# VectorE's order in the second and third expert block: gate product and token low halves first, map building behind them, and the map results read one block later

## The chip, the core and the metric

One core of a Trainium2 chip runs the whole program. The metric is the device time of one execution in microseconds (us). The engines are named as in the profile: PE is TensorE's matmul, PEld its weight load, DVE is VectorE, ACT is ScalarE, POOL is GpSimd, SP is SyncE. Each engine has its own list of instructions; they meet through semaphores only.

## What is computed

A decoder layer on 512 tokens of width 1024: a hybrid mixer, a layer norm, a mixture of experts and a second layer norm. The change lies in the mixture of experts, which is, cut to what matters:

```python
def hierarchical_moe(x, w_rg, b_rg, w_re, b_re, w_up, w_down):
    """Top-1 expert group, then top-2 experts inside that group; SwiGLU experts."""
    xf = x.reshape(bsz * seq, d)
    ...
    gate = jnp.sum(jax.nn.one_hot(expert_id, N_EXPERTS) * weights[..., None], axis=1)
    h = jnp.einsum('nd,edf->nef', xf, w_up)
    h_g, h_u = jnp.split(h, 2, axis=-1)
    h = jax.nn.silu(h_g) * h_u * gate[:, :, None]
    y = jnp.einsum('nef,efd->nd', h, w_down)
```

There are 16 experts in 4 groups, each 1024 -> 2 x 256 -> 1024, and a token goes to two of them. All of it is in float32.

## The kernel before

**Arithmetic.** A float32 operand is split into a high half (rounded to the matmul's float32r, by a cast on ACT) and a low half (the rest, a subtraction on DVE). A product takes three matmul passes: high x high, high x low, low x high. So each weight tile needs a cast on ACT and a subtraction on DVE before PE can use it, and DVE's subtractions ("low halves") are most of its work.

**Blocks.** The experts run as 18 blocks of up to 128 tokens each, in the loop over `b`. The list `seq` names the expert of each block: 0, 1, 2, 3, 4, then 15 twice, 5, 14 twice, and so on. Blocks 0 to 4 have a fixed place in the tables (`NSTAT` = 5, "static"). From block 5 on, the tokens of a block are known only from the "dynamic maps" `ix_x` (which tokens) and `gw_x` (their gate weights), which have to be built on the chip while the first blocks run.

**One block b**, in the order in which the code issues it:

- `up_mm(b)`: 24 matmuls of PE on the tokens `xs` and the up weights `hl` (L109 in the profile, `mm<-hl,xs`).
- `h_ev`: the transposed hidden tile of block b-1 gets its high half (ACT) and its low half (DVE, L83 `hT`).
- `dn_prep`: the down weights of block b-1: casts L1200 (ACT), two low halves L1209 (DVE).
- Up weights of block b+1: four casts L761 (ACT) and four low halves L767 (DVE). Three of the low halves stand here, the fourth is put into the list `tail`.
- `gate_h`: the activation (ACT L1176), then the product with the gate weight (DVE L1177). I call it the gate product of block b.
- `transp(b+1)`: 8 transposes (PE L1162) of the gathered tokens of the next block and their halves (ACT and DVE L83 `xs`).
- `weave(tail)`: what was put into `tail`, on DVE.
- a gather (POOL L1086, an indirect DMA) for block b+4, and a scatter-add (POOL L1233) of an earlier block's result.
- `down_mm(b-1)`: 12 matmuls (PE L1220).
- `h_tr(b)`: two transposes of the hidden tile (PE L1183). They need the gate product of block b. `up_mm(b+1)` stands right behind them on PE.

`weave(chain, fill)` issues the operations of `chain` with those of `fill` spread between them. The stretch is scheduled by hand (`manual_schedule`): the order in the code is the order on each engine.

**The maps.** `order_experts` (L1126 to L1138) and `order_tokens` (L1281 to L1299) are some 30 small DVE operations on tiles of at most 128 x 160. `map_ops` builds the operands of a small matmul: `ohv_x` (L1045) and eight one-hot tiles (L1047). `map_mm` (PE L1055, 8 matmuls into a PSUM tile `aux`) multiplies them. `map_ix` (DVE L1061) turns the result into row numbers `ix_x`, which the gathers for block 5 and later need; `map_gw` (DVE L1066, L1067) gives `gw_x`, which the gate product needs from block 5 on. So DVE feeds `map_mm` and reads its result.

Of the kernel before, what the change touches and what calls it, by code (L numbers as in the profile page):

```python
# [34 lines left out]
NCOLX = NDYN + NSPLIT + NEXTRA  # L35
# [18 lines left out]
def trunk(ctx, tc, x, mem, rows, cols, wz, wkv, pac, pb8, pb2, wax, ws, wo, wr, br, we, out):  # L54
# [88 lines left out]
    def weave(chain, fill=()):  # L143
        done = 0
        for i, f in enumerate(chain):
            f()
            while done * len(chain) < (i + 1) * len(fill):
                fill[done]()
                done += 1
# [100 lines left out]
    with ExitStack() as st_a:  # L250
# [106 lines left out]
        rstd, ops = rstd_ops(mv)  # L357
# [51 lines left out]
        zx, ops = rstd_ops(None, 2, xst[:, :, 2])  # L409
# [87 lines left out]
    with ExitStack() as sc_stack:  # L497
# [15 lines left out]
        for h in range(CH):  # L513
# [19 lines left out]
            for et in range(2):  # L533
                ps = mmps()
                ztile(ps, wq, et)
                b = cc(C_Q + 2 * h + et)
# [227 lines left out]
    def prep_lo(key, i, eng=None, c0=0, c1=1024):  # L764
        t = wus[key][i]
        src = raws[key, i // 2][:, (i % 2) * 1024:(i % 2 + 1) * 1024]
        (eng or dve).tensor_tensor(t[:, 1, c0:c1], src[:, c0:c1], t[:, 0, c0:c1].bitcast(F32), op=ALU.subtract)  # L767
# [291 lines left out]
    def map_ix(ps_, nb, name):  # L1059
        ix = rtile([P, nb], "ix_" + name, I32)  # L1060
        dve.tensor_scalar(ix, ps_[:, :nb], -1.0, None, op0=ALU.add)  # L1061
        return ix
# [20 lines left out]
    def gather(key, ix, b):  # L1083
        xg = xgs[len(xgi) % len(xgs)]
        xgi[key] = xg
        pool.indirect_dma_start(out=xg, out_offset=None, in_=x1_d[:, :],  # L1086
                                in_offset=bass.IndirectOffsetOnAxis(ap=ix[:, b:b + 1], axis=0),
                                bounds_check=T - 1, oob_is_err=False)
# [7 lines left out]
    blk = {}  # L1096
# [164 lines left out]
    def where(b):  # L1261
        p_ = seq[b]
        if p_ < NSTAT:
            return ixs, gws, NS - 1 - p_
        second = b > 0 and seq[b - 1] == p_
        return blk["ixx"], blk.get("gwx"), p_ - NSTAT + (NSPLIT if second else 0)
# [38 lines left out]
    for b in range(nb):  # L1305
        p_ = seq[b]
        nxt = seq[b + 1] if b + 1 < nb else p_
        pu = up_mm(b)
        if b == 0:
            sp.dma_start(seen_d, xgi[1][0:1, 0:4])  # L1310
            for e, u in ((2, 1), (3, 0), (3, 1), (4, 0), (4, 1)):
                load_unit(e, u)
            dn_hi(0, 0)
            dn_hi(0, 1)
            pw = map_mm(ohs_s, NS, 1, 3)
            gws = map_gw(pw, NS, "s")
            h = gate_h(pu, gws, NS - 1)
            hT = h_ev(h_tr(h))
            dn_lo(0, 0, dve, None)
            transp(1)  # L1320
            dn_lo(0, 1, dve, None)
            pdn[0] = down_mm(0, hT)
            scatter(down_ev(pdn[0]), *where(0)[::2])
        elif b > 1:
            hT = h_ev(pth)
        if b == 3:
            blk["ixx"] = map_ix(pix, NCOLX, "x")
            gather(5, *where(5)[::2])
            gather(6, *where(6)[::2])
            weave(vals_x)  # L1330
            pwx = map_mm(ohs_x, NCOLX, 1, 3)
        if b == 4:
            blk["gwx"] = map_gw(pwx, NCOLX, "x")
        ix, gw, c = where(b)
        new = [seq[b - 1]] if b and (b == 1 or seq[b - 2] != seq[b - 1]) else []
        if b == nb - 1:
            break

        def dn_prep():
            for p1 in new:  # L1340
                pl = pools[p_] if nxt != p_ else xp if pools[p_] is hlp else hlp
                for n in range(2):
                    if b > 1:
                        dn_hi(p1, n)
                        dn_lo(p1, n, dve, pl)
                if at[p1] + 3 < E:
                    load_unit(order[at[p1] + 3], 2)

        if b == nb - 2:
            scatter(down_ev(pdn[b - 2]), *where(b - 2)[::2])  # L1350
        dn_prep()
        tail = []
        if b == 1:
            load_unit(order[5], 0)
        if b and nxt != p_:
            for i in range(3):
                prep_hi(nxt, i)
        if 3 < b < nb - 2:
            yb = down_ev(pdn[b - 2])
        held = b > 1 and seq[b - 2] == seq[b - 1]  # L1360
        if b and nxt != p_:
            if not held:
                prep_hi(nxt, 3)
            if b == 1:
                ops = oe_b + order_tokens()
                weave(ops[:8], [lambda i=i, c=c_: prep_lo(nxt, i, None, c, c + 512) for i in range(2) for c_ in (0, 512)])
                weave(ops[8:18], [lambda c=c_: prep_lo(nxt, 2, None, c, c + 512) for c_ in (0, 512)])
                tail = ops[18:] + [lambda: prep_lo(nxt, 3)]
            else:
                ops = []  # L1370
                if b == 2:
                    ohs_x, ops, vals_x = map_ops(blk["px"], blk["ohx"], NCOLX, "x")
                weave(ops[:5] or [lambda: None] * 3, [lambda i=i: prep_lo(nxt, i) for i in range(3)])
                tail = ops[5:] if held else ops[5:] + [lambda: prep_lo(nxt, 3)]
        if b and nxt != p_:
            for i in (2 * at[p_] + 9, 2 * at[p_] + 10):
                if i < 2 * E:
                    load_unit(order[i // 2], i % 2)
        if b:
            h = gate_h(pu, gw, c)  # L1380
        if 0 < b < nb - 1:
            transp(b + 1)
        weave(tail)
        if b + 4 < nb and b not in (1, 2):
            gather(b + 4, *where(b + 4)[::2])
        if b == nb - 2:
            gb2 = mlate.tile([P, 2048], F32, name="raw3")
            g2, b2 = gb2[:, :D], gb2[:, D:]

            def load_gb(eng, i):  # L1390
                r = ROWS.index("ln2_g") + i
                eng.dma_start((g2, b2)[i], rows[r:r + 1, :].to_broadcast([P, D]))

            load_gb(sp, 0)
            load_gb(sp, 1)
        if 3 < b < nb - 2:
            scatter(yb, *where(b - 2)[::2])
        if b == nb - 4:
            oht = mox.tile([P, 4, T], F32R, name="rawx", bufs=2)
            row_hot(oht[:, 0], *where(nb - 3)[::2])  # L1400
        if b == nb - 3:
            for i in range(1, 3):
                row_hot(oht[:, i], *where(nb - 3 + i)[::2])
        if b > 1:
            pdn[b - 1] = down_mm(b - 1, hT)
            if b == nb - 2:
                ys.append(down_split(pdn[b - 1]))
            elif b < 3:
                scatter(down_ev(pdn[b - 1]), *where(b - 1)[::2])
        if b:  # L1410
            pth = h_tr(h)
        if held:
            prep_half(nxt, 3)
        if b == 2:
            pix = map_mm(ohs_x, NCOLX, 0, 1)
    xz = yp.tile([P, NT, D], F32, name="y")
    xs_ = [xz[:, t, :] for t in range(NT)]
    for t in range(NT):
# [167 lines left out]
```

## Time and profile before

| | us |
|---|---|
| median of 3 runs | 917.89 (917.84 to 918.22) |
| the profiled execution, its own time | 920.99 |
| its span, from the first to the last instruction | 919.2 |

The profile is of one execution. Of its span PE is busy 96%, DVE 64% and ACT 50%. The stretch of the change lies between about 718 and 770 us of the span. "Granted clock" is the clock that PE got, as a share of 2.4 GHz: 1.00 is 2.4 GHz and 0.50 is 1.2 GHz. The chain of waits follows back from the last instruction to what released each step, and so lists what set the end. In a timeline row, the bracket says how long the engine had stood idle before that row, and what ended the wait.

### The profile page before, as it was taken

Reading aid. Unit: us, or ns where it says so; the run is one execution under the profiler, and the core shown is the slowest. Engines: PE = TensorE matmul, PEld = TensorE weight load, DVE = VectorE, ACT = ScalarE, POOL = GpSimd, SP = SyncE. Lnnn points to the kernel's source line nnn. Section 1 sums busy time; section 2 is a strip of 40 time slices with the busy share of each in tenths; the row PEclk is TensorE's granted clock in tenths of the full one; section 3 lists DMA queues with packets and bytes.
Section 4 is the critical chain, followed back from the end, with each engine's and each line's share of the span. In section 5 each row is a group of like instructions: output and inputs, shape, how many; then the busy total and the mean of one; then the engine's idle time right before and its main releaser. Section 6 shows DMA issues by size and latency. Waiting matters only on the chain.

```text
span 919.2 us, 11177 instructions
## 1 busy us (share of the span) xinstructions
PE 883.4 (96%) x4272; PEld 733.8 (80%) x4272; DVE 588.8 (64%) x1020; ACT 460.6 (50%) x656; POOL 58.1 (6%) x59
## 2 busy tenths in 40 slices
PE   9999999999999999999999999999998889999991
PEld 5778888889998888888878888788887678888870
DVE  6765773344555543345866865766768887689976
ACT  5545432223444342214678687534204657688942
POOL 0000100000000000000000000000001123233210
PEclk9999999999999999999999999999997989999996
DMA  8313632333322412221313322237673988899544
GB/s 339 123 46 115 218 126 97 112 112 109 121 93 92 142 46 91 102 79 73 129 62 106 138 73 88 92 109 279 229 286 112 409 320 274 269 285 405 146 151 96
DMA packets 29281, 144.70 MB, mean 157 GB/s; under 512 B 5461, under 2 KB 5717, under 8 KB 16166
## 3 DMA queue, kind: packets, MB, share of 16 engines
q1 hardware_dynamic: 21462, 127.25, 37.6%
q0 software_dynamic: 6048, 13.45, 5.8%
q10 hardware_dynamic: 1712, 3.24, 1.1%
q8 instruction: 35, 0.57, 0.3%
q14 instruction: 24, 0.20, 0.1%
HBM read 136.24 MB, written 17.30 MB: 167 GB/s over the span
## 4 chain that ended last, share of the span: by engine, by line
PE 78%; DVE 11%; ACT 5%; DMA 3%; issue 2%; SPq 0%; DVEq 0%; ACTq 0%
PE mm L109 61%; PE mm L1220 4%; PE aux L109 4%; PE mm L308 3%; DVE hl L767 2%; PE aux L1162 1%; DMA x<-in_x_dram 1%; DMA col<-in_cols_dram 1%; ACT hl L82 1%; PE aux L1442 1%; DMA o<-in_we_dram 1%; DVE hl L83 1%; PE aux L464 1%; DVE xs L83 1%; ACT hl L1200 1%
## 5 line engine op out<-in xcount | busy, mean ns | idle before, releaser
L109 PE MATMUL mm<-hl 128*128 128x512 f32 x1416 | 327.6, 390 | 0.2 <-DVE hl L83 0.2
L109 PEld LDWEIGHTS mm<-hl 128*128 128x128 f32 x1416 | 264.7, 188 | 54.6 <-DVE hl L83 0.6
L83 DVE TENSOR_TENSOR hl<-raw,hl 128x1024 fp32r<-128x1024 f32 (+1 forms) x116 | 136.3, 1181 | 136.7 <-ACT hl L82 136.2
L82 ACT CAST hl<-raw 128x1024 fp32r<-128x1024 f32 (+1 forms) x116 | 116.3, 1015 | 126.3 <-PE mm L109 113.8
L109 PE MATMUL mm<-o,hl 128*128 128x512 f32 x624 | 142.9, 389 | 1.2 <-ACT o L82 1.2
L109 PEld LDWEIGHTS mm<-o,hl 128*128 128x128 f32 x624 | 117.1, 188 | 25.8 <-ACT o L82 1.6
L109 PE MATMUL mm<-hl,xs 128*128 128x512 f32 x408 | 99.7, 401 | 0.0
L109 PEld LDWEIGHTS mm<-hl,xs 128*128 128x128 f32 x408 | 77.1, 193 | 15.9
L767 DVE TENSOR_TENSOR hl<-o,hl 128x1024 fp32r<-128x1024 f32 (+1 forms) x45 | 50.3, 1147 | 4.8 <-ACT hl L761 4.7
L1220 PE MATMUL mm<-hl,hT 128*128 128x512 f32 x196 | 49.5, 399 | 0.0
L761 ACT CAST hl<-o 128x1024 fp32r<-128x1024 f32 x42 | 41.9, 1051 | 4.2 <-PE mm L1220 4.2
L1220 PEld LDWEIGHTS mm<-hl,hT 128*128 128x128 f32 x196 | 35.6, 188 | 6.8
L1086 POOL DMA_INDIRECT y<-x_d,ixg x3 | 3.2, 1070 | 594.5 <-DVE rtl L1145 593.9
L224 ACT ACTIVATE gate<-mm,col 128x512 f32<-128x512 f32 x24 | 16.5, 688 | 39.7 <-PE mm L109 39.6
L1209 DVE TENSOR_TENSOR hl<-raw,hl 128x1024 fp32r<-128x1024 f32 x26 | 30.6, 1220 | 3.2 <-PE mm L109 1.6
L1200 ACT CAST hl<-raw 128x1024 fp32r<-128x1024 f32 x32 | 31.9, 1053 | 0.0
L109 PE MATMUL mm<-memT,hl 128*128 128x256 f32 x192 | 27.3, 286 | 0.2 <-ACT memT L82 0.2
L308 PE MATMUL mm<-o,hl 128*128 128x512 f32 x96 | 25.8, 421 | 0.9 <-ACT hl L82 0.6
L109 PEld LDWEIGHTS mm<-memT,hl 128*128 128x128 f32 x192 | 24.9, 191 | 0.9 <-ACT memT L82 0.4
L808 ACT COPY x1T<-aux 128x512 f32<-128x512 f32 x8 | 4.7, 587 | 40.6 <-PE aux L807 25.9
L109 PE MATMUL mm<-hl,yh 128*128 128x512 f32 x96 | 24.4, 400 | 0.0
L109 PE MATMUL mm<-hl,memT 128*128 128x256 f32 x192 | 24.3, 283 | 0.0
(337 smaller groups left out, 1157.8 us busy)
## 6 DMA issues: line engine op xcount, KB each, us to landing
raw<-in_wz_dram SPq DMA_DIRECT2D x30, 1024.0 KB, 4.7
o<-in_we_dram SPq DMA_DIRECT2D x21, 1024.0 KB, 8.0
raw<-in_we_dram SPq DMA_DIRECT2D x18, 1024.0 KB, 7.5
rawx<-in_we_dram SPq DMA_DIRECT2D x9, 1024.0 KB, 7.8
raw<-in_pac_dram SPq DMA_DIRECT2D x8, 1024.0 KB, 4.7
raw<-in_wkv_dram SPq DMA_DIRECT2D x8, 1024.0 KB, 4.7
raw<-in_pb_dram SPq DMA_DIRECT2D x4, 1024.0 KB, 6.2
raw<-in_wo_dram SPq DMA_DIRECT2D x4, 1024.0 KB, 4.9
```

What stands on the lines that cost most here:

```text
L82: act.copy(hi, src)
L83: dve.tensor_tensor(lo, src, hi.bitcast(F32), op=ALU.subtract)
L109: pe.matmul(ps, lhsT=a(sa_), rhs=b(sb_), start=first and i == 0, stop=last and i == 2)
L224: act.activation(store[j], ps, AF.Sigmoid, bias=cc(C_M + br_i * 8 + j))
L308: pe.matmul(ps, lhsT=xT(k, slice(t * P, (t + 1) * P))(sx), rhs=wv[2 * n + k // 4, k // 2 % 2][:, sw, k % 2, :], start=i == 0, stop=i == 23)
L464: pe.matmul(pv[:, ch * P:(ch + 1) * P], lhsT=v[:, ch, g * P:(g + 1) * P], rhs=wst[:, g, :], start=True, stop=True)
L761: act.copy(t[:, 0], raws[key, i // 2][:, (i % 2) * 1024:(i % 2 + 1) * 1024])
L767: (eng or dve).tensor_tensor(t[:, 1, c0:c1], src[:, c0:c1], t[:, 0, c0:c1].bitcast(F32), op=ALU.subtract)
L1162: pe.transpose(ps[:, j * P:(j + 1) * P], xg[:, k * P:(k + 1) * P], ident)
L1200: act.copy(dnh[key][:, :, n * 512:(n + 1) * 512], dn_half(key, n))
L1209: eng.tensor_tensor(dnl[key][n], dn_half(key, n), dnh[key][:, :, ns].bitcast(F32), op=ALU.subtract)
L1220: pe.matmul(ps, lhsT=hT[:, sa_, f, :], rhs=dn[sb_][:, f, :], start=i + f == 0, stop=i + f == 3)
```

## The change

Three things move; no operation is added or removed.

1. In block 1 the rest of `order_experts` and all of `order_tokens` but its first eight operations go from ahead of the gate product into `tail`, behind the low halves of up weight tiles 2 and 3.
2. In block 2 the making of the map operands (`ohv_x`, eight L1047), until now woven between the up weights' low halves, goes into `tail`, behind all four low halves.
3. `map_mm` for `ix_x` moves from the end of block 2 to behind `up_mm(3)`, with its reading `map_ix` right behind it. The other half (`vals_x`, `map_mm` for `gw_x`) moves from block 3 to behind `up_mm(4)`, with `map_gw` right behind it.

```diff
@@ -1324,12 +1324,12 @@
         if b == 3:
-            blk["ixx"] = map_ix(pix, NCOLX, "x")
+            blk["ixx"] = map_ix(map_mm(ohs_x, NCOLX, 0, 1), NCOLX, "x")
             gather(5, *where(5)[::2])
             gather(6, *where(6)[::2])
+        if b == 4:
             weave(vals_x)
             pwx = map_mm(ohs_x, NCOLX, 1, 3)
-        if b == 4:
             blk["gwx"] = map_gw(pwx, NCOLX, "x")
@@ -1364,14 +1364,13 @@
             if b == 1:
                 ops = oe_b + order_tokens()
                 weave(ops[:8], [lambda i=i, c=c_: prep_lo(nxt, i, None, c, c + 512) for i in range(2) for c_ in (0, 512)])
-                weave(ops[8:18], [lambda c=c_: prep_lo(nxt, 2, None, c, c + 512) for c_ in (0, 512)])
-                tail = ops[18:] + [lambda: prep_lo(nxt, 3)]
+                tail = [lambda i=i: prep_lo(nxt, i) for i in (2, 3)] + ops[8:]
             else:
-                ops = []
+                weave([lambda: None] * 3, [lambda i=i: prep_lo(nxt, i) for i in range(3)])
+                tail = [] if held else [lambda: prep_lo(nxt, 3)]
                 if b == 2:
                     ohs_x, ops, vals_x = map_ops(blk["px"], blk["ohx"], NCOLX, "x")
-                weave(ops[:5] or [lambda: None] * 3, [lambda i=i: prep_lo(nxt, i) for i in range(3)])
-                tail = ops[5:] if held else ops[5:] + [lambda: prep_lo(nxt, 3)]
+                    tail += ops
@@ -1411,8 +1410,6 @@
         if held:
             prep_half(nxt, 3)
-        if b == 2:
-            pix = map_mm(ohs_x, NCOLX, 0, 1)
```

How the lists of instructions change, at three places. First DVE in block 1, as a piece of the difference (`h<-h,gw_s,mm` is the gate product of block 1, `xs` the token low halves of block 2, `hl<-o` low halves of block 2's up weights):

```order
 L1135 TENSOR_TENSOR tab<-ntot,nx 128x16
+L1177 SCALAR_TENSOR_TENSOR h<-h,gw_s,mm 128x256
+L83 TENSOR_TENSOR xs<-aux,xs 128x512 x2
+L767 TENSOR_TENSOR hl<-o,hl 128x1024 x2
 L1136 TENSOR_REDUCE eidf<-scr 128x7
-L767 TENSOR_TENSOR hl<-o,hl 128x512
 L1137 COPY eidf<-ntot 128x1
 L1138 TENSOR_SCALAR eix<-eidf 128x8
 L1281 TENSOR_TENSOR scr<-oh,tab 128x128 x2
 L1284 TENSOR_REDUCE t_5544<-scr 128x8
```

The gate product and the token low halves now stand ahead of the small operations from L1136 on.

Second, PE from the end of block 2 to block 4 (`aux<-ident,h` is `h_tr`, `aux<-ident,y` is `transp`, 128x20 is the map for `ix_x`, 128x40 that for `gw_x`):

```order
 L1183 MATMUL aux<-ident,h 128x128 x2
+L109 MATMUL mm<-hl,xs 128x512 x24
 L1055 MATMUL aux<-ohv_x,yb 128x20 x8
+L1162 MATMUL aux<-ident,y 128x128 x8
+L1220 MATMUL mm<-hl,hT 128x512 x12
+L1183 MATMUL aux<-ident,h 128x128 x2
 L109 MATMUL mm<-hl,xs 128x512 x24
 L1055 MATMUL aux<-ohv_x,yb 128x40 x8
```

Each of the two map matmuls now stands one `up_mm` later than before.

Third, DVE from block 3 on, first as it was:

```order
L83 TENSOR_TENSOR hT<-aux,hT 128x256
L1061 TENSOR_SCALAR ix_x<-aux 128x20
L1045 TENSOR_TENSOR ohv_x<-ohx,val 128x8x20 x2
L1209 TENSOR_TENSOR hl<-raw,hl 128x2x512 x2
L767 TENSOR_TENSOR hl<-o,hl 128x1024 x3
L1177 SCALAR_TENSOR_TENSOR h<-h,gw_s,mm 128x256
L83 TENSOR_TENSOR xs<-aux,xs 128x512 x2
L767 TENSOR_TENSOR hl<-o,hl 128x1024
L83 TENSOR_TENSOR hT<-aux,hT 128x256
L1066 COPY gw_x<-aux 128x20
L1067 TENSOR_TENSOR gw_x<-gw_x,aux 128x20
L1209 TENSOR_TENSOR hl<-raw_5523,hl 128x2x512 x2
```

and as it is now:

```order
L83 TENSOR_TENSOR hT<-aux,hT 128x256
L1061 TENSOR_SCALAR ix_x<-aux 128x20
L1209 TENSOR_TENSOR hl<-raw,hl 128x2x512 x2
L767 TENSOR_TENSOR hl<-o,hl 128x1024 x3
L1177 SCALAR_TENSOR_TENSOR h<-h,gw_s,mm 128x256
L83 TENSOR_TENSOR xs<-aux,xs 128x512 x2
L767 TENSOR_TENSOR hl<-o,hl 128x1024
L83 TENSOR_TENSOR hT<-aux,hT 128x256
L1045 TENSOR_TENSOR ohv_x<-ohx,val 128x8x20 x2
L1066 COPY gw_x<-aux 128x20
L1067 TENSOR_TENSOR gw_x<-gw_x,aux 128x20
L1209 TENSOR_TENSOR hl<-raw_5523,hl 128x2x512 x2
```

On DVE the two reads of the maps, L1061 and L1066, keep their places in blocks 3 and 4, ahead of the down weights' low halves L1209, the up weights' low halves L767 and the gate product L1177 of the same block; what they read is now made by PE behind `up_mm` of the same block.

## Rows read from the trace of the kernel before

**Rows 1.** The page: span, then busy time (share of span) of PE.
```profile
span 919.2 us, 11177 instructions
PE 883.4 (96%) x4272; PEld 733.8 (80%) x4272; DVE 588.8 (64%) x1020; ACT 460.6 (50%) x656; POOL 58.1 (6%) x59
```

**Rows 2.** Timeline of PE, 722 to 775: start, duration, engine, line; idle before.
```profile
727.30 0.44 PE L1183 MATMUL aux<-ident,h 128*128 128x128 f32 x2 [2.17 <-DVE h L1177]
727.50 5.74 PE L109 MATMUL mm<-hl,xs 128*128 128x512 f32 x24
...
738.97 0.44 PE L1183 MATMUL aux<-ident,h 128*128 128x128 f32 x2 [2.12 <-DVE h L1177]
...
740.36 1.03 PE L1055 MATMUL aux<-ohv_x,yb 128*128 128x20 f32 x4 [0.59 <-DVE yb L1047]
```

**Rows 3.** Chain of waits, 715 to 920: start, us, what.
```profile
738.52 0.39 DVE h L1177
...
740.36 1.03 PE aux L1055 x4
741.39 7.99 PE mm L109 x24
749.38 0.80 PE aux L1055 x8
750.18 0.94 PE aux L1162 x8
751.12 2.79 PE mm L1220 x12
753.91 0.22 PE aux L1183 x2
754.12 5.48 PE mm L109 x24
...
763.23 0.22 PE aux L1183 x2
```

**Rows 4.** Windows of 1 us: PE, PEld, DVE, ACT, POOL busy; PEclk, DMA share, GB/s.
```profile
739.00:740.00 1.00, 0.77 (x6) 0.67 (x6) 1.00 (x2) 0.56 (x2) 0.80 (x1) 0.80 1.07 377
...
746.00:747.00 1.00, 1.00 (x5) 0.77 (x4) 1.00 (x2) 0.00 (x0) 0.00 (x0) 0.78 0.95 328
```

**Rows 5.** Timeline of all engines, 698 to 728 (first two) and 726 to 775.
```profile
723.79 0.17 DVE L1135 TENSOR_TENSOR tab<-ntot,nx 128x16 f32<-128x16 f32 x1
...
724.30 0.39 ACT L1176 ACTIVATE h<-mm 128x256 f32<-128x256 f32 x1 [1.11 <-PE mm L109]
...
734.02 0.32 DVE L1045 TENSOR_TENSOR ohv_x<-ohx,val 128x160 fp32r<-128x160 f32 x1
...
736.72 0.47 DVE L1047 TENSOR_SCALAR yb<-iof,px 128x128 fp32r<-128x128 f32 x2
```

**Rows 6.** Timeline of all engines, 711 to 715, DVE's part.
```profile
712.21 0.17 DVE L1066 COPY gw_s<-aux 128x6 f32<-128x6 f32 x1 [0.70 <-PE aux L1055]
...
714.10 0.42 DVE L83 TENSOR_TENSOR hT<-aux,hT 128x256 fp32r<-128x256 f32 x1 [0.94 <-ACT hT L82]
714.44 1.22 DVE L1209 TENSOR_TENSOR yb<-raw,hl 128x1024 fp32r<-128x1024 f32 x1
```

**Rows 7.** Timeline of all engines, 726 to 775, DVE's rows of blocks 3 and 4.
```profile
742.29 0.16 DVE L1061 TENSOR_SCALAR ix_x<-aux 128x20 int32<-128x20 f32 x1
...
744.24 2.36 DVE L1209 TENSOR_TENSOR hl<-raw,hl 128x1024 fp32r<-128x1024 f32 x2 [1.32 <-ACT hl L761]
...
746.52 3.49 DVE L767 TENSOR_TENSOR hl<-o,hl 128x1024 fp32r<-128x1024 f32 x3
...
749.92 0.47 DVE L1177 SCALAR_TENSOR_TENSOR h<-h,gw_s,mm 128x256 f32<-128x256 f32 x1
...
755.11 0.18 DVE L1067 TENSOR_TENSOR gw_x<-gw_x,aux 128x20 f32<-128x20 f32 x1
```

**Rows 8.** All instructions on the tile ix_x: its gathers and scatters to landing.
```profile
DMA to landing us min/median/max: 4.8/6.3/10.9
```

## The prediction

> **What bounds the kernel now.** I read the page first: PE is busy for 883.4 of 919.2 us [rows 1], so only what PE waits for can matter. The next view is PE's timeline through the expert blocks: where it stands idle, and on whom it waits. There are three waits between 725 and 741, each on DVE: 2.17 us ahead of `h_tr(1)`, 2.12 ahead of `h_tr(2)`, both for the gate product L1177, and 0.59 in the map matmul, for the one-hot tiles L1047 [rows 2]. From 741.39 on the chain of waits is PE alone, block after block [rows 3], so whatever is won or lost up to block 4 stays to the end. The third view is the windows of 1 us: the granted clock is 1.00 until 739.6 and 0.50 (1.2 GHz) from there to 746.4. I get the two instants from the mixed values, 0.80 and 0.78 [rows 4]: 0.5 for a share x of the microsecond gives 1 - x/2, so x is 0.4 in each. `up_mm(3)` lies in the slow stretch and takes 7.99 us, where `up_mm(4)` takes 5.48 [rows 3]. PE had just stood still for 2.12 us when the clock fell. After the 2.17 us ahead of block 2 it did not fall: `up_mm(2)` took 5.74 on the same timeline [rows 2], against 8.0 in the slow stretch.
>
> **Block 1.** DVE ends L1135 at 723.96, and ACT has the activation of block 1 at 724.69 [rows 5]. In the new order the gate product comes next, so it starts at about 724.7. It takes 0.39 [rows 3], and `h_tr(1)` goes at 725.15 instead of 727.30: 2.15 us won, PE's first wait gone. `up_mm(2)` moves up as much.
>
> **Block 2 gives it back.** DVE has no slack here: from 723.96 until the gate product of block 2 at 738.52 [rows 3, 5] it is busy throughout. The new order takes `ohv_x` (0.23 to the next start) and four one-hot tiles (0.39 for two [rows 5], so 0.8) out of that stretch: 1.0 us less. It adds 0.75 us in which DVE waits for the activation at 724.69, and the small operations, most of them depending on the one before, now run without a low half between them; I put 0.2 on that. That makes the gate product of block 2 come at about 738.5, as before. PE gets there earlier and waits longer, about 3 us in place of 2.1. So the 2.15 us are worth nothing by themselves.
>
> **The map matmul leaves its place.** Before, it stood between `h_tr(2)` and `up_mm(3)`; now `up_mm(3)` starts at 739.2 instead of 741.39. I let the clock fall at 739.6 and rise at 746.4 as before, since PE's wait ahead of it is longer, not shorter. By 739.6 0.4 us of the 5.48 are done, in the slow stretch 6.8 / 2 = 3.4, and the other 1.7 at full clock end at 748.1. Behind it comes the map matmul, 0.80 [rows 3] at full clock, to 748.9. In the old order this place held the other map matmul, from 749.38 on, so PE is 1.3 us ahead.
>
> **DVE stands still for the map, in block 3.** The order on DVE is `hT`, `map_ix`, two L1209, three L767, gate product. `map_ix` can't start before 748.9, while DVE is ready at about 743.5 (the last low half of block 2, nine map operations and `hT` behind 738.5: 0.4 + 1.2 + 1.15 + 1.9 + 0.35). What waits behind it is not only what needs the map. That DVE passes nothing ahead is shown by the low half L1209 at 714.44: its inputs were there while DVE stood idle for 0.70 and 0.94 us on other tiles, and it ran behind both [rows 6]. After the map DVE needs 0.17 for `map_ix`, 2.28 for two L1209 (744.24 to 746.52), 3.40 for three L767 (to 749.92 [rows 7]), 0.39 for the gate product: 6.3 us with the hand-overs, to 755.2. PE has 0.94 of transposes and 2.79 of `down_mm(2)` [rows 3], 3.7 us, and then waits 2.6. In the kernel before, the same 5.7 us of low halves ran from 744.24 on under `up_mm(3)`; that cover is gone. `h_tr(3)` comes at 755.2 instead of 753.91: 1.3 late.
>
> **The same again in block 4.** `up_mm(4)` takes 0.22 + 5.48 from there, to 760.9; the second map matmul 0.80, to 761.7 (it stood in block 3 before). `map_gw` is two small operations of about 0.2 [rows 7], so DVE needs 6.5 to the gate product, and `h_tr(4)` comes at 768.2. Before it came at 763.23 [rows 3]: 5.0 late. In this block PE waits 2.8. Nothing later gives it back: behind block 4 PE was already the only link of the chain.
>
> **The gathers** of blocks 5 and 6 need `ix_x` and go at 749.1 instead of 742.7. The slowest of its gathers and scatters landed 10.9 us after issue [rows 8], so by 760.0; `transp(5)` stands at 761.7. No wait. The weight loads are issued when low halves free their buffers, so they move with DVE by the same 5 us, and no ACT cast of blocks 3 to 15 waited for a load; I cost them at nothing.
>
> **The clock, the cost that has no row of its own.** Two new waits, 2.6 and 2.8 us, are longer than the one after which the clock held (2.17) and the one after which it fell (2.12, with the 0.59 soon after) [rows 2]. One fall costs up to 3.4 us: 6.8 us at half clock, if PE has work throughout, and `up_mm(4)` with what follows is such work; some of it is hidden where PE then waits for DVE anyway, so I take 3.3. From below the bound is nothing. I hold a fall behind either wait for a little likelier than not, and one fall in all for the likeliest.
>
> **The sum** against the profiled execution (920.99): 5.0 without a further fall, 8.3 with one, 11.6 with two. I carry these to the median. The median, 917.89, lies 3.10 below the profiled execution. That is close to what its fall at 739.6 cost (7.99 - 5.48 = 2.5, and 0.6 in the map matmul), so the timed runs may not have had this fall; the new order, with its wait of 3 us there, would then add it, which is the same one further fall.
>
> **The rivals.**
> - *No further fall*: 917.89 + 5.0 = 922.9. For it: PE stood 2.17 us at full clock without a fall.
> - *Two further falls*: 917.89 + 11.6 = 929.5. For it: both new waits are longer than any that kept the clock in these blocks.
> - *Faster*: `up_mm(3)` keeps 2.4 GHz, and DVE's low halves fit under PE. The place is the stretch from the map matmul to the gate product in blocks 3 and 4. `up_mm(3)` then ends at 744.7, the map at 745.5, `h_tr(3)` comes at 749.2 and `h_tr(4)` at 749.2 + 0.22 + 5.48 + 0.80 + 3.7 = 759.4: 3.9 won, 914.0. It decides from the point where DVE gets from the map to the gate product in 3.7 us rather than 6.3; the durations in rows 7 speak against it.
> - *Nothing*: the waits are covered, the clock falls as before. `h_tr(3)` at 752.6, `h_tr(4)` at 762.8: 0.4 won, 917.5. It would need the moved reads not to hold DVE up, which is the case in which the change does not do on DVE what its list says.
> - *The old fall goes*: DVE's waits stay, but the clock holds in `up_mm(3)`. Map at 745.5, `h_tr(3)` 751.8, `h_tr(4)` 764.8: 1.6 late, 919.5.
> - *Late gathers*: POOL issues them from 749.1 on beside DVE's unbroken low halves, where before DVE was idle until 744.24 [rows 7]. `transp(5)` waits from the point where a landing takes more than 12.6 us. If one came as far behind the slowest as that lies behind the median (10.9 + 4.6 = 15.5 [rows 8]), it would wait 2.9: 925.8. Against it: the gathers of this kernel ran beside DVE's low halves in most blocks and landed within 10.9. The Trainium skill's page "SBUF — State Buffer", section "SBUF: two separate sides", says that VectorE and GpSimd share a port pair as an exclusive lock, so that a DMA issued by GpSimd can wait for a VectorE instruction to end, and gives 620 ns alone against 3100 ns beside one. By an estimate from that page the slowest would land 2.5 us later, 0.8 behind the slack, and the time would be 923.7.
>
> **How the numbers follow.** Chances: one further fall 0.37, none 0.24, two 0.20, late gathers 0.02, old fall gone 0.06 (half of it within 0.2%), nothing 0.06, faster 0.05. A measurement of this kernel can tell about 0.2% (1.8 us) from no change. The likeliest is 917.89 + 8.3 = 926.2. The range from 921.5 to 930.5 holds no, one and two falls with about 1 us for my DVE times, and leaves out 0.17 and a small tail. Slower by over 0.2%: 0.37 + 0.24 + 0.20 + 0.02 + 0.03 = 0.86; within: 0.09; faster: 0.05.
>
> **What would show it.** In the profile after: `h_tr(1)` near 725.2 with no wait; the gate product of block 2 still near 738.5; DVE idle for some 5 us ahead of L1061, and again ahead of L1066, released by PE L1055; PE idle 2.6 to 2.8 us ahead of `h_tr(3)` and `h_tr(4)`, on DVE L1177; L1162 of block 5 without a wait. I am wrong if DVE runs L1209 and L767 of block 4 ahead of L1061, if the gate product of block 2 comes two or more us earlier, or if the clock behaves otherwise: each fall is a stretch at 0.50 of about 6.8 us.

## The result: slower by 5.3 us

| | before | after |
|---|---|---|
| median of 5 runs | 918.20 us (917.84 to 918.67) | 923.51 us (921.88 to 928.13) |
| profiled execution | 920.99 us, span 919.2 | 921.88 us, span 920.1 |
| mean granted clock of the profiled execution | 0.982 | 0.986 |

The ratio after to before is 1.0057, with an interval of 1.0041 to 1.0073: small, but clear of the noise. The time lies in the predicted range, 2.7 us below the predicted 926.2 and 0.6 above the 922.9 of the rival without a further clock fall. The two profiled executions lie only 0.9 us apart: the one of before is among its slowest (918.2 is its median), the one of after is its fastest. So the two traces must not be compared by their spans. I compare waits, and the distance from one `h_tr` to the next. Block 1 begins about 1.2 us earlier in the trace of after, because the stretch at 0.50 that both traces show near 700 us lasted 6.8 us in that execution and 10.2 in the one of before (`up_mm(0)` took 7.29 us against 8.59); instants of the two traces are not compared either. One of the six executions of the kernel after in the last experiment took 1779.23 us, at a granted clock of 1.00 and for a reason that the record doesn't show; it is counted in no figure below.

The page of after, the rows that answer to [rows 1]:

```profile
span 920.1 us, 11178 instructions
...
PE 882.1 (96%) x4272; PEld 732.3 (80%) x4272; DVE 588.3 (64%) x1019; ACT 460.5 (50%) x656; POOL 61.7 (7%) x59
```

PE, DVE and ACT have no more work than before (POOL has 3.6 us more, and is idle for 93% of the span), so the time was lost standing still. DVE even has one instruction fewer: the low half of up weight tile 2 in block 1, two operations of 512 columns before, is one of 1024 now, so the change doesn't only move things. The timeline of PE in after, 722 to 785 us, answers to [rows 2 and 3] (start, duration, engine, line, operation; in brackets the idle time before it and who ended that):

```profile
724.03 0.44 PE L1183 MATMUL aux<-ident,h 128*128 128x128 f32 x2
724.23 5.94 PE L109 MATMUL mm<-hl,xs 128*128 128x512 f32 x24
...
738.01 0.44 PE L1183 MATMUL aux<-ident,h 128*128 128x128 f32 x2 [2.83 <-DVE h L1177]
738.21 5.71 PE L109 MATMUL mm<-hl,xs 128*128 128x512 f32 x24
743.75 0.96 PE L1055 MATMUL aux<-ohv_x,yb 128*128 128x20 f32 x8
...
751.13 0.41 PE L1183 MATMUL aux<-ident,h 128*128 128x128 f32 x2 [2.70 <-DVE h L1177]
751.30 5.70 PE L109 MATMUL mm<-hl,xs 128*128 128x512 f32 x24
756.84 0.96 PE L1055 MATMUL aux<-ohv_x,yb 128*128 128x40 f32 x8
757.65 1.09 PE L1162 MATMUL aux<-ident,y 128*128 128x128 f32 x8
...
764.44 0.66 PE L1183 MATMUL aux<-ident,h 128*128 128x128 f32 x2 [2.90 <-DVE h L1177]
764.75 6.83 PE L109 MATMUL mm<-hl,xs 128*128 128x512 f32 x24
```

The four rows of L1183 are `h_tr(1)` to `h_tr(4)`. The wait of 2.17 us ahead of `h_tr(1)` is gone, the one ahead of `h_tr(2)` has grown from 2.12 to 2.83, and there are two new ones, 2.70 ahead of `h_tr(3)` and 2.90 ahead of `h_tr(4)`, all released by the gate product on DVE. `transp(5)`, the L1162 at 757.65, waits for nothing, so the later gathers cost nothing. With the waits of 0.44 and 0.40 in `down_mm(1)`, PE stands still for 9.3 us here (2.83 + 2.70 + 2.90 + 0.44 + 0.40), where before it was 4.9 (2.17 + 2.12 + 0.59): 4.4 more.

Why the gate product is late shows in the timeline of DVE in after, 722 to 775 us, which answers to [rows 7] (same columns):

```profile
737.49 0.47 DVE L1177 SCALAR_TENSOR_TENSOR h<-h,gw_s,mm 128x256 f32<-128x256 f32 x1
...
744.75 0.18 DVE L1061 TENSOR_SCALAR ix_x<-aux 128x20 int32<-128x20 f32 x1 [2.32 <-PE aux L1055]
744.84 2.35 DVE L1209 TENSOR_TENSOR hl<-raw,hl 128x1024 fp32r<-128x1024 f32 x2
747.11 3.49 DVE L767 TENSOR_TENSOR hl<-o,hl 128x1024 fp32r<-128x1024 f32 x3
750.51 0.47 DVE L1177 SCALAR_TENSOR_TENSOR h<-h,gw_s,mm 128x256 f32<-128x256 f32 x1
...
757.84 0.18 DVE L1066 COPY gw_x<-aux 128x20 f32<-128x20 f32 x1 [3.72 <-PE aux L1055]
758.15 2.35 DVE L1209 TENSOR_TENSOR hl<-raw,hl 128x1024 fp32r<-128x1024 f32 x2
760.42 3.48 DVE L767 TENSOR_TENSOR hl<-rawx,hl 128x1024 fp32r<-128x1024 f32 x3
763.82 0.47 DVE L1177 SCALAR_TENSOR_TENSOR h<-h,gw_s,mm 128x256 f32<-128x256 f32 x1
```

DVE stands idle for 2.32 us ahead of L1061 and 3.72 ahead of L1066, until PE has made the map. Five low halves and the gate product are queued behind each read, and none of them needs the map. From the start of the read to that of the gate product DVE takes 5.8 and 6.0 us. In the same time PE has only the transposes and `down_mm` left.

The clock, in windows of 1 us of after (us, then PE, PEld, DVE, ACT, POOL busy; then the granted clock, DMA share, GB/s), answering to [rows 4]:

```profile
763.00:764.00 1.00, 0.00 (x0) 0.00 (x0) 1.00 (x2) 0.00 (x0) 0.10 (x1) 0.86 1.04 426
764.00:765.00 1.00, 0.56 (x3) 0.59 (x4) 1.00 (x3) 0.00 (x0) 0.00 (x0) 0.50 0.99 410
...
766.00:767.00 1.00, 1.00 (x3) 0.75 (x3) 1.00 (x3) 1.00 (x2) 0.00 (x0) 0.50 0.98 361
767.00:768.00 1.00, 1.00 (x5) 0.80 (x4) 1.00 (x1) 1.00 (x3) 0.00 (x0) 0.94 1.03 356
```

PE stands still through the whole microsecond from 763, during its third wait; the clock falls at 763.7 and is back at 767.1. That is a stretch of 3.4 us at 1.2 GHz. It costs 6.83 - 5.72 = 1.1 us in `up_mm(5)`. In `up_mm(3)`, which ran at half clock before, the clock held: 5.71 us, right behind a wait of 2.83.

### The profile page after: what moved, and what is told of

Its sections match the earlier page's. It is cut to its first block, busy times and chain, and to the rows that moved or that the text cites. A ratio compares the mean times of both kernels' runs of the same rounds, so it can differ in the third digit from the quotient of the medians.

```text
span 920.1 us, 11178 instructions
## 1 busy us (share of the span) xinstructions
PE 882.1 (96%) x4272; PEld 732.3 (80%) x4272; DVE 588.3 (64%) x1019; ACT 460.5 (50%) x656; POOL 61.7 (7%) x59
## 5 line engine op out<-in xcount | busy, mean ns | idle before, releaser
L767 DVE TENSOR_TENSOR hl<-o,hl 128x1024 fp32r<-128x1024 f32 (+1 forms) x44 | 49.8, 1168 | 4.8 <-ACT hl L761 4.7
L1209 DVE TENSOR_TENSOR hl<-raw,hl 128x1024 fp32r<-128x1024 f32 x26 | 30.6, 1217 | 1.5 <-PE mm L109 1.2
```

The source lines that it names most:

```text
L1209: eng.tensor_tensor(dnl[key][n], dn_half(key, n), dnh[key][:, :, ns].bitcast(F32), op=ALU.subtract)
```

## The experiments

The change has three parts: the **first** puts the gate product and token low halves ahead in block 1, the **second** does the same in block 2 (the map operations go behind), and the **third** has both map matmuls and their reads one block later. Theory 1 is that of the prediction: DVE, an in-order engine, waits for a map that PE makes late, and everything queued behind the read waits too. The rivals are the clock and the gathers.

**Only the reads moved back (e1).** The kernel after, but `map_ix` with its two gathers stands behind the down weights' low halves of block 3, and `map_gw` at the end of block 4. The map matmuls stay where the change put them:

```diff
         if b == 3:
-            blk["ixx"] = map_ix(map_mm(ohs_x, NCOLX, 0, 1), NCOLX, "x")
-            gather(5, *where(5)[::2])
-            gather(6, *where(6)[::2])
+            pix = map_mm(ohs_x, NCOLX, 0, 1)
         if b == 4:
             weave(vals_x)
             pwx = map_mm(ohs_x, NCOLX, 1, 3)
-            blk["gwx"] = map_gw(pwx, NCOLX, "x")
...
         dn_prep()
+        if b == 3:
+            blk["ixx"] = map_ix(pix, NCOLX, "x")
+            gather(5, *where(5)[::2])
+            gather(6, *where(6)[::2])
...
         weave(tail)
+        if b == 4:
+            blk["gwx"] = map_gw(pwx, NCOLX, "x")
```

> The changed kernel, with the two reads of the maps moved on VectorE: map_ix behind the down weights' low halves of block 3, map_gw behind all low halves of block 4. The matmuls of the maps stay where the change put them. Theory (VectorE waits in its list for the map matmul, and the low halves and the gate product behind it are late): PE's waits ahead of h_tr(3) and h_tr(4), 2.7 and 2.9 us in the changed kernel, shrink to under 0.8 us each, and the time comes to 917 to 919. Rival 1 (the clock falls are the loss, from PE's long wait ahead of h_tr(2), which stays): 921 to 924. Rival 2 (the map is late for the gathers): a wait ahead of the transposes of block 5, 921 to 924.

Measured: 917.31 us (915.64 to 919.11, 12 runs) against 918.84 of before beside it; ratio 0.9982, 0.9972 to 0.9992. Three operations moved on DVE (and two gathers on POOL with them), and the loss of 5.3 us became a gain of 1.5. PE's timeline of this kernel shows the wait ahead of `h_tr(2)` unchanged, 0.43 left ahead of `h_tr(3)`, and none ahead of `h_tr(4)` (the row at 759.97):

```profile
738.80 0.44 PE L1183 MATMUL aux<-ident,h 128*128 128x128 f32 x2 [2.83 <-DVE h L1177]
...
749.71 0.41 PE L1183 MATMUL aux<-ident,h 128*128 128x128 f32 x2 [0.43 <-DVE h L1177]
...
759.97 0.38 PE L1183 MATMUL aux<-ident,h 128*128 128x128 f32 x2
```

DVE's timeline of the same kernel shows the low halves under `up_mm(3)`, the read behind them without a wait (there is no bracket), and the gate product 3.5 us behind the read (745.59 to 749.09). `up_mm(3)` runs from 739.00 to 744.76 here, so the inputs of L1209 are there before the map is made; in after the same operations stood behind the read until the map was there. That is how the rows show that DVE passes nothing ahead:

```profile
743.14 2.34 DVE L1209 TENSOR_TENSOR hl<-raw,hl 128x1024 fp32r<-128x1024 f32 x2
745.59 0.18 DVE L1061 TENSOR_SCALAR ix_x<-aux 128x20 int32<-128x20 f32 x1
745.68 3.49 DVE L767 TENSOR_TENSOR hl<-o,hl 128x1024 fp32r<-128x1024 f32 x3
749.09 0.47 DVE L1177 SCALAR_TENSOR_TENSOR h<-h,gw_s,mm 128x256 f32<-128x256 f32 x1
```

The windows of 10 us show the same in sum (columns as above). First this kernel:

```profile
740.00:750.00 10.00, 9.57 (x52) 7.88 (x51) 9.89 (x19) 6.69 (x9) 3.66 (x2) 1.00 0.88 307
750.00:760.00 10.00, 10.00 (x55) 8.44 (x54) 10.00 (x15) 8.28 (x12) 3.12 (x4) 1.00 0.96 349
```

and then the kernel after:

```profile
740.00:750.00 10.00, 8.43 (x46) 6.90 (x44) 7.68 (x17) 5.89 (x8) 4.20 (x3) 1.00 0.71 250
750.00:760.00 10.00, 8.87 (x49) 7.59 (x50) 6.25 (x12) 8.27 (x12) 2.45 (x2) 1.00 0.80 304
```

DVE, the third of the busy times, is busy for 19.9 of 20 us here and for 13.9 in after; PE gets 19.6 us of work done in place of 17.3. The wait ahead of `h_tr(2)` is the same in both, so it isn't the cause; nor are the gathers, which went as late as in after.

**The third part alone, on the kernel before (e2).**

```diff
         if b == 3:
-            blk["ixx"] = map_ix(pix, NCOLX, "x")
+            blk["ixx"] = map_ix(map_mm(ohs_x, NCOLX, 0, 1), NCOLX, "x")
...
+        if b == 4:
             weave(vals_x)
             pwx = map_mm(ohs_x, NCOLX, 1, 3)
-        if b == 4:
             blk["gwx"] = map_gw(pwx, NCOLX, "x")
...
-        if b == 2:
-            pix = map_mm(ohs_x, NCOLX, 0, 1)
```

> The kernel before with the third part of the change alone: the two map matmuls and their reads one up_mm later; block 1 and block 2 as before. Theory (this part carries the whole loss, since in block 2 nothing is won): 922 to 925, with VectorE idle ahead of L1061 and L1066 and PE waiting 2.5 to 3 us ahead of h_tr(3) and h_tr(4). Rival (the sorting and map operations run in a row, without low halves between them, are the loss): 917 to 919.

Measured: 923.45 us (922.36 to 924.25, 6 runs); ratio 1.0050, 1.0036 to 1.0064. The third part alone costs as much as the whole change. PE's waits ahead of `h_tr(3)` and `h_tr(4)` are those of after, 2.70 and 2.92, and the clock fell behind the first of them: `up_mm(4)` took 6.90. In this trace it also fell behind the wait of 2.19 ahead of `h_tr(1)` (`up_mm(2)` 7.32), where it held in before behind 2.17.

**The first part alone (e4), and the first and second (e3).** The first part on the kernel before:

```diff
-                weave(ops[8:18], [lambda c=c_: prep_lo(nxt, 2, None, c, c + 512) for c_ in (0, 512)])
-                tail = ops[18:] + [lambda: prep_lo(nxt, 3)]
+                tail = [lambda i=i: prep_lo(nxt, i) for i in (2, 3)] + ops[8:]
```

> The kernel before with the first part of the change alone: in block 1 the gate product and the low halves come ahead of the rest of the sorting. Theory (VectorE has no slack from block 1 to the gate product of block 2): the 2.2 us won at h_tr(1) are lost at h_tr(2), where PE waits about 4 us; VectorE adds 0.95 us of its own (its wait for the activation of block 1, and small operations in a row): 919 to 921. Rival (the won 2.2 us stay): 915.5 to 916.5.

Measured: 920.65 us (919.39 to 922.92, 12 runs); ratio 1.0019, 1.0010 to 1.0028. With the second part:

```diff
-                ops = []
+                weave([lambda: None] * 3, [lambda i=i: prep_lo(nxt, i) for i in range(3)])
+                tail = [] if held else [lambda: prep_lo(nxt, 3)]
                 if b == 2:
                     ohs_x, ops, vals_x = map_ops(blk["px"], blk["ohx"], NCOLX, "x")
-                weave(ops[:5] or [lambda: None] * 3, [lambda i=i: prep_lo(nxt, i) for i in range(3)])
-                tail = ops[5:] if held else ops[5:] + [lambda: prep_lo(nxt, 3)]
+                    tail += ops
```

> The kernel before with the first and second part of the change: gate product and low halves first in blocks 1 and 2; the map matmuls and their reads where they were. Theory: PE's wait ahead of h_tr(1) goes, that ahead of h_tr(2) grows to 2.8 us, and the map matmul ahead of up_mm(3) waits 3.5 us for the one-hot tiles; up_mm(3) starts about 1.8 us later than before: 919 to 923, the upper end if the clock falls more often. Rival (low halves first is a gain, and only the third part spoils it): 913 to 916.

Measured: 922.26 us (921.03 to 922.85, 7 runs); ratio 1.0035, 1.0022 to 1.0047. So the first part loses time where it stands, and the second, added to it, doesn't win it back (it was not run by itself). The rows of PE, first with the first part alone, show what takes the place of the wait removed at `h_tr(1)`:

```profile
733.48 0.73 PE L1220 MATMUL mm<-hl,hT 128*128 128x512 f32 x2 [0.47 <-DVE hT L83]
734.61 2.10 PE L1220 MATMUL mm<-hl,hT 128*128 128x512 f32 x8 [0.40 <-DVE hl L1209]
740.56 0.44 PE L1183 MATMUL aux<-ident,h 128*128 128x128 f32 x2 [3.85 <-DVE h L1177]
...
742.81 8.54 PE L109 MATMUL mm<-hl,xs 128*128 128x512 f32 x24
```

and with both parts:

```profile
739.15 0.44 PE L1183 MATMUL aux<-ident,h 128*128 128x128 f32 x2 [2.83 <-DVE h L1177]
...
742.00 1.85 PE L1055 MATMUL aux<-ohv_x,yb 128*128 128x20 f32 x8 [2.41 <-DVE yb L1047]
743.70 7.85 PE L109 MATMUL mm<-hl,xs 128*128 128x512 f32 x24
```

The 2.17 us come back and more: PE waits 3.85 ahead of `h_tr(2)`, where it was 2.12, and 0.47 and 0.40 in `down_mm(1)`, where it waited for nothing, 2.60 more in all. The second part takes one microsecond off the 3.85, but the wait in the map matmul, 0.61 with the first part alone, becomes 2.41, since the one-hot tiles now come after the low halves. Behind these waits `up_mm(3)` ran partly at half clock in both executions (8.54 and 7.85), as it did in before. This is why the second part needs the third: only with the map matmul out of the way can `up_mm(3)` start at `h_tr(2)`. The third part in its turn loses it on the reads.

**One read at a time (e5 and e6).** The kernel after, with `map_gw` alone moved back (as in the first experiment):

> The changed kernel with map_gw alone moved on VectorE, behind all low halves of block 4. Theory (each of the two reads costs its own wait): PE's wait ahead of h_tr(4), 2.9 us, goes; that ahead of h_tr(3), 2.7, stays: 920 to 921.5, about 2.9 under the changed kernel. Rival (the first read alone is the cause, block 4 is only late after block 3): the wait ahead of h_tr(4) stays, 923 to 924.

Measured: 921.79 us (921.16 to 923.48, 6 runs), 0.3 above what was expected; ratio 1.0042, 1.0028 to 1.0057. The wait ahead of `h_tr(4)` is gone, that ahead of `h_tr(3)` is 2.70 as in after. Then the kernel after with `map_ix` and its gathers alone moved back, behind the down weights' low halves:

> The changed kernel with map_ix alone moved on VectorE, behind the two down low halves of block 3. Theory: the wait ahead of h_tr(3) falls from 2.7 to 0.4 us, that ahead of h_tr(4), 2.9, stays: 920.5 to 922, about 2.3 under the changed kernel. Rival (block 4 is late only after block 3): both waits go, 917 to 918.

Measured: 921.78 us (918.88 to 925.66, 12 runs); ratio 1.0038, 1.0021 to 1.0056. The rows of PE and DVE in this kernel show that each read has its own wait:

```profile
751.76 0.41 PE L1183 MATMUL aux<-ident,h 128*128 128x128 f32 x2 [0.43 <-DVE h L1177]
...
765.08 0.41 PE L1183 MATMUL aux<-ident,h 128*128 128x128 f32 x2 [2.90 <-DVE h L1177]
```

```profile
758.48 0.18 DVE L1066 COPY gw_x<-aux 128x20 f32<-128x20 f32 x1 [3.73 <-PE aux L1055]
```

The distances from one `h_tr` to the next, worked out from the starts of the L1183 rows on PE's timelines, put the prices side by side (us). The last column is the pace of the later blocks, 9.3 us, where no fall reaches into it. "(fall)" marks a distance in which `up_mm` ran partly at half clock:

| | 2 to 3 | 3 to 4 | 4 to 5 |
|---|---|---|---|
| before | 14.77 (fall) | 9.33 | 9.33 |
| after | 13.12 | 13.31 | 10.60 (fall) |
| `map_gw` moved back | 14.72 (fall) | 11.52 (fall) | 9.32 |
| `map_ix` moved back | 10.85 | 13.32 | 9.37 |
| both moved back | 10.91 | 10.26 | 9.33 |

By these rows the read L1061 costs 13.12 - 10.91 = 2.2 us and L1066 13.31 - 10.26 = 3.05, 5.3 together. By the ratios to before, `map_gw` alone gives 0.15% (1.4 us), `map_ix` alone 0.19% (1.7 us), and both 0.75% (6.9 us). The intervals of the first two overlap that of after (1.0041 to 1.0073), so what each read costs rests on the traces; only the gain from both is clear of the noise in the times as well. By these figures `map_gw` alone gives 1.6 us less than its price, `map_ix` 0.5 less, and both together 1.6 more. Each of the two kernels with one read moved still has a long wait in block 3 or 4, and the trace of the first has two falls behind its waits. The runs with `map_ix` moved back point to the clock: six took 918.88 to 920.96 us, with a mean granted clock of 0.986 to 0.988 over the whole run, and six took 922.59 to 925.66, with 0.981 to 0.984; no run lies within 0.8 us of the median. Where in those runs the clock fell isn't on record, so that the difference is clock remains likely and not shown.

**The clock's share (e7).** The kernel after, with eight matmuls, whose result nobody reads, put ahead of `h_tr(2)`, `h_tr(3)` and `h_tr(4)`, where PE waits anyway:

```diff
+        if b in (2, 3, 4):
+            ps_ = auxps()
+            for i in range(8):
+                pe.matmul(ps_, lhsT=hT[:, 0, 0, :], rhs=dnh[seq[b - 1]][:, 0, :512], start=True, stop=True)
         if b:
             pth = h_tr(h)
```

> The changed kernel with 8 matmuls (128x512, into a PSUM tile that nobody reads) ahead of h_tr(2), h_tr(3) and h_tr(4): 1.8 us of work inside each of PE's three waits. VectorE's order is untouched, so no wait ends earlier. Theory 1 (part of the loss, and the spread of the runs from 921.9 to 928.1, is the clock that falls behind a long wait): the granted clock stays 1.00 from 726 on, the runs lie within 1.5 us, median 920 to 922. Theory 2 (the clock is a small part): the median stays at 923 to 924. In both, PE's waits shrink to about 1 us each, and h_tr(3) and h_tr(4) come no earlier than with the full clock before.

Measured: 922.00 us (920.27 to 923.14, 7 runs); ratio 1.0038, 1.0025 to 1.0051. In the trace the granted clock is 1.00 in every window from 720 to 780, `up_mm(3)` to `up_mm(5)` take 5.74 or 5.75, and DVE's waits on the map stay (2.36 and 3.70). So with the clock kept in these blocks the change still costs 3.3 us against the 918.74 of before beside it. Against the 923.51 of after, the falls are worth about 1.5 (by the two ratios 1.7). That is an estimate: the intervals of the two ratios overlap. The expectation on the spread failed: the runs lie 2.9 us apart and not 1.5. Stretches at 0.50 between 698 and 719, 10.2 us in all, are left in this kernel's trace and may be the reason.

**How far the clock goes in the better kernel (e8 and e9).** The kernel of the first experiment, with eight unread matmuls ahead of `h_tr(2)` and seven in the routing stage ahead of `rank_mm`:

> The kernel of e1 (reads later) with 8 such matmuls ahead of h_tr(2), and 7 in the routing stage, where PE waits 1.65 us for the counts of the last token tile and the clock falls just behind (698.6 in the profile before). Theory 1 (the clock falls where PE has had little to do, and idle time filled with work keeps it): 1.00 from 690 to 890, the slow stretch of 6.8 to 10.2 us around 700 goes: 912 to 914.5. Theory 2 (the light matmuls of the routing stage, not the wait, let it fall): the fall at 698 stays, 916 to 918.

Measured: 915.99 us (915.29 to 917.61, 8 runs); ratio 0.9974, 0.9963 to 0.9985. Against the 917.31 of the first experiment that is 1.3 us won (0.7 by the two ratios, whose intervals overlap), where theory 1 expected 2.8 to 5.3. The matmuls in the routing stage can't be judged by the traces. The profiled execution of the first experiment, which has none of them, shows 1.00 from 690 to 710 as well, and its only stretch at 0.50 before the last 20 us comes with a wait of 3.75 us ahead of `h_tr(0)` (one window of 10 us and PE's row):

```profile
700.00:710.00 10.00, 7.96 (x42) 6.73 (x40) 9.64 (x36) 6.75 (x9) 3.21 (x3) 1.00 0.38 107
```

```profile
711.71 0.69 PE L1183 MATMUL aux<-ident,h 128*128 128x128 f32 x2 [3.75 <-DVE h L1177]
```

Here a stretch of the same length, 6.8 us, lies from 709.6 to 716.4, with a wait of 3.86 (`h_tr` is L1186 in this kernel):

```profile
711.39 0.66 PE L1186 MATMUL aux<-ident,h 128*128 128x128 f32 x2 [3.86 <-DVE h L1180]
```

The expectation had compared with the fall at 698.6 in the trace of before, and that fall is not in every execution. Twelve more unread matmuls stand ahead of `h_tr(0)` in the next kernel:

> The kernel of e8 with 12 more such matmuls (2.7 us) ahead of h_tr(0), where PE in e8 waits 3.9 us for the gate product of block 0 and the clock fell at 709.6 behind that wait. Theory (a fall is what a long wait brings, and it moves from wait to wait): no stretch at 0.50 before the last 20 us, runs within 1.5 us, median 913 to 915. Rival (in this stretch VectorE sets the time, the clock is hidden): 915.5 to 916.5, as e8.

Measured: 915.42 us (914.34 to 915.62, 5 runs); ratio 0.9953, 0.9940 to 0.9966. Its windows of 10 us, two of them, have the granted clock at 1.00, and so have all others from 700 to 780:

```profile
730.00:740.00 10.00, 8.16 (x39) 5.90 (x38) 9.76 (x21) 4.49 (x8) 1.80 (x1) 1.00 0.96 375
...
750.00:760.00 10.00, 10.00 (x55) 8.49 (x54) 10.00 (x14) 8.07 (x13) 3.43 (x3) 1.00 1.01 390
```

This is the fastest kernel of the study by its median, 0.47% below the kernel before, with runs 1.3 us apart. But taking away a whole stretch at half clock gave 0.6 us by the medians, 1.9 by the ratios, and the time is 0.4 above what was expected. The traces show where the rest went. From `h_tr(0)` to `h_tr(1)` it is 12.01 us in place of 12.88, 0.9 won, and PE, at full clock, now waits for DVE's low halves in `down_mm(0)`, where it waited for nothing in the kernel with the fall:

```profile
714.87 0.73 PE L1223 MATMUL mm<-yb,hT 128*128 128x512 f32 x2 [0.25 <-DVE yb L1212]
...
717.20 0.73 PE L1223 MATMUL mm<-yb,hT 128*128 128x512 f32 x2 [0.67 <-DVE yb L1212]
```

**The kernel after once more (e10)**, beside that one on the same chip:

> The changed kernel itself, once more, beside the runs of the kernel before on the same chip, since its first five runs spread over 6 us. Expected from the first ones: median 922.5 to 924.5, spread above 3 us, no less than e7 (922.0), which has the same waits with the clock kept.

Measured: 923.60 us (923.13 to 925.04) in the five runs that are counted; ratio 1.0050, 1.0037 to 1.0063. The median is the expected one, the spread isn't: 1.9 us, where above 3 was expected. The three waits are 2.84, 2.70 and 2.90, as in the first trace, and the clock fell again behind the third (6.88 for `up_mm(5)`) and held behind the other two.

## Why the prediction held, and which term was too large

- **Block 1.** Right. `h_tr(1)` goes without a wait, 12.11 us behind `h_tr(0)` in place of 14.08: 2.0 won, where 2.15 were predicted.
- **Block 2 gives it back.** Right. The wait was to be about 3 us and is 2.83. The first part alone shows the mechanism without the others: 2.17 us less ahead of `h_tr(1)`, 1.73 more ahead of `h_tr(2)`, 0.87 more in `down_mm(1)`, and no gain. The prediction didn't see these last waits (0.44 and 0.40 in after).
- **DVE stands still for the map.** Right in mechanism and, for PE, in size: waits of 2.6 and 2.8 were predicted ahead of `h_tr(3)` and `h_tr(4)`, and they are 2.70 and 2.90. Moving the two reads takes the whole loss away. DVE's own idle time was to be some 5 us twice; it is 2.32 and 3.72. For the first, the prediction ran `up_mm(3)` at half clock, and it ran at full clock in this execution. The second 5 doesn't follow from the prediction's own instants: its gate product of block 3 starts at about 754.8, DVE takes 3.6 us from there to the read (750.51 to 754.12 in after), and its map is there at 761.7, which makes 3.3.
- **The 5.0 us for the waits** were right within a microsecond, but they hang on what the clock does in before. Taken from the distances between the `h_tr`, with 3.1 us for the fall in before (the prediction's price for it) and 1.3 for the one in after left out, the change costs 5.8 us: -2.0 from `h_tr(0)` to `h_tr(1)` (12.11 for 14.08), 2.3 to `h_tr(2)` (13.98 for 11.67), 1.45 to `h_tr(3)` (13.12 for 14.77 less 3.1), 4.0 to `h_tr(4)`. Against the median of before it is 3.3 (the run with the unread matmuls). The two fit if a part of before's executions have a fall of their own: 922.0 less 5.8 is 916.2, and the fastest run of before took 916.39. That is argued, not shown.
- **Nothing gives it back.** Right: from `h_tr(5)` on the blocks go at the same pace in both kernels, 9.33 us up to the last two.
- **The gathers** cost nothing, as predicted. They were issued from 745.19 on and landed within 10.2 us, and `transp(5)` waits for none.
- **The clock is the term that was mis-sized.** The likeliest case was one further fall of 3.3 us. The runs give about 1.5 for the falls in these blocks (923.51 against 922.00 with the unread matmuls), which the noise doesn't separate from nothing. Two assumptions failed. The first is that a stretch at half clock lasts about 6.8 us: the one behind `h_tr(4)` lasted 3.4 and cost 1.1. The second is that the clock falls in `up_mm(3)` as it did in the trace of before: it held in both traces of after, behind waits of 2.83 and 2.84. It did fall there when PE had waited 2.82 in the kernel with `map_gw` moved back (`up_mm(3)` 7.30). Whether it falls differs from one execution of a kernel to the next, so one trace's fall should not have been carried over.
- **The profiled execution and the median.** The prediction took the 3.10 us between 920.99 and 917.89 for the cost of the fall at 739.6. The later runs of the kernel before bear this out in size only: they go from 916.39 to 920.99 in the same order of instructions. That it was this fall is not shown, since the runs without a profile don't tell where their clock fell. The traces speak against a part of it: from the start of the last `h_tr` to the end of the span the profiled execution of before takes 35.3 us, and the eleven others take 33.1 to 34.8, 33.9 at the mean, with the same busy time of every engine. So, by an estimate from these, some 1.4 of the 3.10 us lie behind the last block and not at 739.6.

So the prediction named the right stretch, the right waits and their size, and its time was 2.7 us too high by the clock term. The time came out near the rival that it gave 0.24, not near its likeliest case with 0.37. That rival, without a further fall, is off by 0.6 alone, yet part of that nearness is luck: its 5.0 us were carried from the profiled execution to a median whose runs fall in other places, and by the estimate above some 1.5 of the 5.3 us are falls.

## What to carry to other kernels

When a result is made later, move its reader on the in-order engine behind all work that doesn't need it, or the whole queue waits: here the same change with three operations placed later went from 5.3 us lost to 1.5 us won. Before taking a wait out of a stretch, add up the engine that releases it: where that engine has no gap up to the next hand-over, the wait only moves. And TensorE's waits of 2.1 to 3.9 us were paid for twice here in some executions and not in others, so one should not read the price of a fall, or what removes it, from a single trace.

## What the runs showed of the hardware

- A wait of PE of 2.7 to 2.9 us was followed by half clock in some executions and not in others: behind `h_tr(3)` the clock held in both traces of after (`up_mm(4)` 5.70 and 5.74) and fell with the same wait of 2.70 in the third part alone (6.90) and with `map_gw` moved back (6.86). The nine traces without unread matmuls ahead of `h_tr(1)` to `h_tr(4)` have 18 waits of 2.1 to 3.9 us there; half clock began in or behind nine of them, before the next `h_tr`.
- With unread matmuls in place of most of such a wait the granted clock stayed at 1.00: of the waits of 2.83, 2.70 and 2.90 there were 1.01, 0.79 and 1.12 left, and no fall from 720 to 780. The same holds for the wait ahead of `h_tr(2)` in e8 and the two filled ones in e9, so for six of six; against the nine of 18 it is likely, and not proved, that the matmuls kept it.
- The indirect gathers on POOL took 1.78 and 1.93 us beside DVE's low halves in after. The Trainium skill's page "SBUF — State Buffer", section "SBUF: two separate sides", says that a DMA issued by GpSimd can wait for a VectorE instruction to end, and gives about 620 ns alone and 3100 ns beside a VectorE copy. The low halves are subtractions and not copies, and the rows don't show such a wait beside them: the second gather of before ran beside the low halves L1209 (744.24 to 746.52 [rows 7]) and took 1.01 us, no more than the one ahead of it, 1.11, most of which fell into DVE's idle time. What made the two of after longer stays open. The slowest landing was not later for it: 10.2 us, with 7.0 at the median, against 10.9 and 6.3 [rows 8]. POOL's rows, first of before:

```profile
742.72 1.11 POOL L1086 DMA_INDIRECT y<-x_d,ix_x  x1 [2.92 <-DVE ix_x L1061]
744.14 1.01 POOL L1086 DMA_INDIRECT y<-x_d,ix_x  x1 [0.30 <-PE mm L109]
```

and of after:

```profile
745.19 1.78 POOL L1086 DMA_INDIRECT y<-x_d,ix_x  x1 [7.29 <-DVE ix_x L1061]
747.27 1.93 POOL L1086 DMA_INDIRECT y<-x_d,ix_x  x1 [0.30 <-issue]
```
